# A one-layer GLA and pooling backbone on one core: attention order shifted by half a head, gates broadcast through DRAM, held weight units loaded earlier, modulation products redistributed

## The chip, the cores and the metric

One core of one Trainium2 chip runs the whole program. The metric is device microseconds of an execution, as the median of several runs. The profile is of one execution, and its own time stands beside its span below.

## The reference, cut to what matters

One layer over 256 latent tokens and 256 context tokens of width 2048, all float32:

```
mods (6 x 2048)  = silu(c) @ w_ada + b_ada              (and for c_ctx)
h_lat = x*(1+sc_m) + sh_m;   h_ctx the same with c_ctx
q,k,v,g,a,p,bg   = split(h @ w_in)                      4 heads, HEAD_K 256, HEAD_V 512
o     = gated linear attention, both directions, chunks of 64;
        latent scans start from the context's final states
y_gla = (rmsnorm(o)*gain * silu(g)) @ w_gla_out
y_pool= (grouped (box mean of p - p) @ w_pool_group) * scale @ w_pool_out
mix   = (sigmoid(bg1)*y_gla + sigmoid(bg2)*y_pool) @ w_out
x     = LN(ALPHA*x + gt_m*mix)
ffn   = (silu(z@w1) * (z@w2)) @ w_ffn_out,   z = x*(1+sc_f) + sh_f,   width 5632
out   = LN(ALPHA*x + gt_f*ffn)
```

Only the latent stream is returned. The two gates gt_m and gt_f are rows of 2048 numbers that multiply every token's row.

## The kernel before, in words

Weights come from DRAM in units of 128 x 1024 float32 (512 KB), all issued from SyncE's queue (`raw_unit`, L91), which issues in order. ScalarE rounds a unit to fp32r (`hi`, L97), VectorE takes the rest (`lo`, L98), and TensorE multiplies in three passes: hi by hi, hi by lo, lo by hi. Raw, hi and lo have three buffers each, so weights are prepared up to three units ahead of TensorE. `nat_block` (L143) has the tokens as the stationary operand and two PSUM banks out of the pool "d" of four; a unit is 12 matmuls of 512 columns. `ws_tile` (L116) has the weights as the stationary operand; a unit is 8 matmuls of 512 columns and 8 of 256. Each takes a callback `after` that is called behind each unit: `hooks` (L639) makes one from a table {unit number, counted from 0: what to do}.

The order of instructions on each engine is laid out at build time by a planner, by priority among those whose inputs it reckons to be ready. Priority is the order in which the program issues them, less a bonus inside `tc.high_priority` (the splits of `weights` have 200, the norms 300). `tc.issue_after(i)` keeps an instruction behind i on its engine. On the chip each engine then goes through its list in order.

The stages, with their starts in the profiled execution: modulation and v (0), k of latent and context (233), first q half (331), attention with the g blocks and the p blocks (345 to 590), bg, w_gla_out and w_pool_out in 16 tiles `ct` (590, L737), w_o in four column blocks (907), the FFN's first product in 44 tiles (1019, L901), its second in four column blocks (1500).

Attention: `front(h)` (L479) is a generator with stages between its `yield`s. For direction d it makes decay products (two matmuls L503, ScalarE exponentials, a scan on VectorE, products with k), yields, then products with q (L558 to L564), score matmuls (L571 to L583) and their evacuation, yields, and the same for d = 1. `back(h)` (L604) multiplies the scores with v (L609 to L611), norms with RMS and gates with g (L616 to L622), yields, then transposes o (L628) and evacuates it. For each head the loop (L671) starts the front of h + 1, issues the PV matmuls of h ahead of the g block of h + 1, and lets hooks place the rest: transposes behind unit 1, both remaining stages up to d = 1's k products behind unit 3, the last one behind unit 6.

Modulation products (`ada`, L255): 96 units of w_adaT (512 KB, SyncE's queue, L268), each multiplied with silu(c) on VectorE and summed (L270). `ADA` (L43) says how many are called where: in the modulation stage, behind k tiles (4 each, 3 buffers), in bg tiles (3 each, 2 buffers; the rest behind the last). There are none from the first q half to the end of attention. Behind them `add_mods` fills `fcol`, which holds the gates as columns (128 x 16).

Gates: `bcast_cols` (L780) turns a column form into a tile of 128 x 2048 that has the gate row in every partition: VectorE makes 8 diagonal tiles from the identity (L789), TensorE multiplies each with ones (L791), ScalarE evacuates (L792). It is called behind the first column block of w_o and, for the second gate, in FFN tile 41. `residual` (L808) needs it.

Held blocks: the last column block of w_o (8 units) and the last four units of w_ffn_out are split into buffers of their own and then multiplied part by part (`PARTS`, L823): tokens 0 to 127 first, then tokens 128 to 255 in two halves of 256 columns, so that the norm of the first tokens runs beside the matmuls of the others (`held_block`, L825). Their loads and splits are issued together when the block begins. `rows` (L802) broadcasts the LayerNorm vectors on POOL's queue; the first call stands in the third w_o block.

Of the kernel before, what the change touches and what calls it, by code (L numbers as in the profile page):

```python
# [8 lines left out]
F32 = mybir.dt.float32  # L9
# [33 lines left out]
ADA = ({8: 1, 12: 2}, 4, 3)  # L43
# [15 lines left out]
def trunk(ctx, tc, small, masks, xT, ctxT, x_nat, lnrows, wdec, pmat, c_row,  # L59
# [83 lines left out]
    def nat_block(srcs, acts, k0=0, after=None, last=None, pre=None, cols=None):  # L143
# [20 lines left out]
        return outs  # L164

# [61 lines left out]
    with ExitStack() as c1:  # L227
# [251 lines left out]
        def front(h):  # L479
# [6 lines left out]
            kv = kh.rearrange("p c (t n i) -> p c t n i", t=2, n=2)  # L486
            for d in range(2):
# [67 lines left out]
                yield  # L555
# [48 lines left out]
        def back(h, g, PT, PC):  # L604

            os = [bank("g") for _ in range(2)]
            for t in range(2):
                for j in range(2):
                    PE.matmul(os[t], PC[:, j, t * P:(t + 1) * P], vc[h][:, j, :], start=(j == 0), stop=False)  # L609
                PE.matmul(os[t], PT[:, t, :], vl[h][:, t, :], start=False, stop=False)  # L610
                PE.matmul(os[t], PT[:, 2 + (1 - t), :], vl[h][:, 1 - t, :], start=False, stop=True)  # L611
# [27 lines left out]
        def hooks(at):  # L639

            n = [0]

            def call():
                at.get(n[0], lambda: None)()
                n[0] += 1
            return call

# [38 lines left out]
        ada_pool.append((py, "ra", NRA))  # L686
# [88 lines left out]
    onesf = p2.tile([P, 512], F32, tag="rt", bufs=NRT, name="onesf")[:, :P]  # L775
    V.memset(onesf, 1.0)
    onesq = p2.tile([P, P], F32R, tag="onesq", name="onesq")
    S.activation(onesq, onesf, AF.Copy)

    def bcast_cols(i):  # L780

        gt = p2.tile([P, D], F32, tag="gt", name=nm("gt"))
        fs = p2.tile([P, 2, 16], F32R, tag="fs", name=nm("fs"))
        split(fcol[:, i, :], fs[:, 0, :], fs[:, 1, :])
        for b in range(4):
            o = bank("g")
            for j in range(2):
                dg = p2.tile([P, 4, P], F32R, tag="rt", bufs=NRT, name=nm("dg"))
                V.tensor_tensor(dg, ident.unsqueeze(1).to_broadcast([P, 4, P]),  # L789
                                fs[:, j, 4 * b:4 * b + 4].bitcast(F32).unsqueeze(2).to_broadcast([P, 4, P]), op=ALU.mult)  # L790
                PE.matmul(o, onesq, dg.rearrange("p a b -> p (a b)"), start=(j == 0), stop=(j == 1))  # L791
            S.activation(gt[:, b * 512:(b + 1) * 512], o, AF.Copy)  # L792
# [32 lines left out]
    def held_block(srcs, dst, acts, k0, kend, outs, bst, norm, finish):  # L825

        ws = []
        for src, (hi, lo) in zip(srcs, dst):
            r = raw_unit(src)
            split(r, hi, lo)  # L830
            ws.append((hi, lo))
# [15 lines left out]
    bst = p2.tile([P, 2, 8, 6], F32, tag="bst", name="bst1")  # L847
    for b in range(3):
        outs = nat_block([w_o[8 * b + i] for i in range(8)], m_s)
# [12 lines left out]
    hold = p2.tile([P, 2 * NF, T], F32R, tag="hid", name="hold")  # L862
    hold = hold.rearrange("p a b -> p (a b)")
# [13 lines left out]
    def finish_mix(t):  # L877
        for b in range(4):
# [4 lines left out]
            for j in range(4):  # L883
# [10 lines left out]
    held_block([w_o[24 + i] for i in range(8)],  # L894
               [(hold[:, 2 * U * i:2 * U * i + U], hold[:, 2 * U * i + U:2 * U * i + 2 * U]) for i in range(8)],
               m_s, 0, KT - 1, None, bst, norm_mix, finish_mix)
# [43 lines left out]
    bst = p2.tile([P, 2, 8, 6], F32, tag="bst", name="bst2")  # L940
    for b in range(3):
        outs = nat_block([w_fo[22 * b + i] for i in range(22)], hid_s)
        for t in range(2):
            residual(b, t, outs[t], bst)
# [4 lines left out]
    def finish_ffn(t):  # L949
        mean, rs = mv_rs[t]  # L950
        for b in range(4):
# [6 lines left out]
    outs = nat_block([w_fo[66 + i] for i in range(18)], [hid_s[t] for t, _, _ in PARTS], last=NF - 1,  # L958
                     cols=[c for _, *c in PARTS])
    hold = [hcp.tile([P, 4 * U], F32R, tag="hc", name=nm("hold")) for i in range(2)]  # L960
    held_block([w_fo[84 + i] for i in range(4)],
# [127 lines left out]
```

## Time and profile before

| | |
|---|---|
| time, median of 3 runs | 1768.76 us (1768.55 to 1773.19) |
| profiled execution, its own time | 1772.31 us |
| its span | 1770.5 us |
| TensorE matmul busy | 1730.5 us (98%) |
| VectorE busy | 1170.1 us (66%) |
| ScalarE busy | 800.3 us (45%) |
| GpSimd busy | 11.5 us (1%) |
| mean granted TensorE clock | 0.992 |
| DMA | 393 MB, 222 GB/s over the span |

Times are counted from the first instruction. A matmul's busy time overlaps the next one's, so a busy TensorE is not one at its peak: the distance between two starts tells its pace. An idle time is put down to whatever ended it. A group's "idle before" is the idle time of its engine just ahead of it.

### The profile page before, as it was taken

What the parts mean: (1) busy time and instruction counts of PE and PEld (TensorE: products, weight loads), DVE (VectorE), ACT (ScalarE), POOL (GpSimd) and SP (SyncE); (2) the same over time, 40 slices, a digit from 0 to 9 for tenths busy, and PEclk for the clock granted to TensorE, in tenths of its full rate; (3) what the DMA queues carried; (4) which work ended last, traced back from release to release, by engine and by line L of the source; (5) the groups of instructions that cost most, each with busy time, mean ns of one, the idle gap of its engine ahead of it and who ended that gap; (6) DMA issues with size and microseconds to landing.
All of it is one profiled execution on the core that took longest, in us unless ns stands there. A gap on an engine that the chain in (4) does not pass through costs nothing.

```text
span 1770.5 us, 24390 instructions
## 1 busy us (share of the span) xinstructions
PE 1730.5 (98%) x9407; PEld 1451.1 (82%) x9407; DVE 1170.1 (66%) x1661; ACT 800.3 (45%) x1173; POOL 11.5 (1%) x28
## 2 busy tenths in 40 slices
PE   9999999999999999999999899999999999999996
PEld 5667888887777888888887788888888888888886
DVE  3667866667875677777776756666666666554455
ACT  2223132565874544444444554445444444443332
POOL 0000010000000000000000000000000000000000
PEclk9999999999999999999999999999999999999998
DMA  9797757443334478777785445577777766555553
GB/s 391 292 354 259 258 210 278 159 157 126 110 120 178 157 267 284 267 258 275 278 306 192 155 166 188 186 264 246 248 236 248 233 236 221 192 192 194 196 190 120
DMA packets 109059, 393.26 MB, mean 222 GB/s; under 512 B 12144, under 2 KB 12272, under 8 KB 108432
## 3 DMA queue, kind: packets, MB, share of 16 engines
q1 hardware_dynamic: 107424, 384.25, 62.4%
q0 software_dynamic: 1520, 7.47, 1.2%
q8 instruction: 73, 1.20, 0.3%
q14 instruction: 42, 0.34, 0.1%
HBM read 389.58 MB, written 2.10 MB: 221 GB/s over the span
## 4 chain that ended last, share of the span: by engine, by line
PE 87%; DVE 6%; ACT 3%; DMA 2%; issue 2%; SPq 0%; ACTq 0%; DVEq 0%
PE ps L127 34%; PE ps L131 18%; PE ps L157 10%; PE ps L160 10%; PE ps L158 10%; PE ps L293 2%; DVE lo L98 1%; DMA raw<-in_w_o 1%; ACT hi L97 1%; DMA raw<-in_w_fi 1%; PE ps L581 1%; DMA rw<-in_w_sh_sc 1%; PE ps L571 0%; PE ps L409 0%; PE ps L709 0%
## 5 line engine op out<-in xcount | busy, mean ns | idle before, releaser
L98 DVE TENSOR_TENSOR lo<-raw,hi 128x1024 fp32r<-128x1024 f32 x510 | 623.7, 1224 | 432.9 <-ACT hi L97 420.8
L97 ACT ACTIVATE hi<-raw 128x1024 fp32r<-128x1024 f32 x510 | 539.2, 1058 | 674.0 <-PE ps L127 275.1
L127 PE MATMUL ps<-h,hi 128*128 128x512 f32 x1408 | 353.4, 392 | 0.8 <-DVE h L98 0.8
L127 PEld LDWEIGHTS ps<-h,hi 128*128 128x128 f32 x1408 | 253.3, 189 | 46.5 <-DVE h L98 1.2
L127 PE MATMUL ps<-hl,hi 128*128 128x512 f32 x768 | 210.3, 392 | 0.0
L131 PEld LDWEIGHTS ps<-h,lo 128*128 128x128 f32 x1408 | 192.5, 190 | 13.9
L131 PE MATMUL ps<-h,lo 128*128 128x256 f32 x1408 | 196.8, 282 | 0.0
L127 PEld LDWEIGHTS ps<-hl,hi 128*128 128x128 f32 x768 | 139.4, 189 | 25.3
L157 PE MATMUL ps<-hi,hid 128*128 128x512 f32 (+1 forms) x372 | 134.9, 369 | 0.0
L158 PE MATMUL ps<-hi,hid 128*128 128x512 f32 (+1 forms) x372 | 134.0, 369 | 0.0
L157 PE MATMUL ps<-hi,hl 128*128 128x512 f32 x320 | 128.7, 403 | 2.7 <-ACT hi L97 2.7
L158 PE MATMUL ps<-hi,hl 128*128 128x512 f32 x320 | 126.6, 396 | 0.0
L270 DVE SCALAR_TENSOR_TENSOR ra<-ra,silb 128x1024 f32<-128x1024 f32 x96 | 114.4, 1221 | 13.0 <-DMA ra<-in_w_adaT 12.9
L131 PE MATMUL ps<-hl,lo 128*128 128x256 f32 x768 | 120.5, 282 | 0.0
L131 PEld LDWEIGHTS ps<-hl,lo 128*128 128x128 f32 x768 | 111.7, 190 | 6.9
L160 PE MATMUL ps<-lo,hl 128*128 128x512 f32 x320 | 93.0, 391 | 0.1
L160 PE MATMUL ps<-lo,hid 128*128 128x512 f32 x372 | 90.6, 369 | 0.0
L157 PEld LDWEIGHTS ps<-hi,hid 128*128 128x128 f32 x372 | 69.8, 188 | 12.1 <-DVE xt L812 0.2
L158 PEld LDWEIGHTS ps<-hi,hid 128*128 128x128 f32 x372 | 70.0, 188 | 11.9
L157 PEld LDWEIGHTS ps<-hi,hl 128*128 128x128 f32 x320 | 60.3, 189 | 22.5 <-issue 5.2
L348 DVE TENSOR_TENSOR v<-ps,v 128x512 f32<-128x512 f32 x80 | 50.7, 685 | 39.8 <-PE ps L160 39.7
L160 PEld LDWEIGHTS ps<-lo,hid 128*128 128x128 f32 x372 | 66.2, 188 | 11.9
(259 smaller groups left out, 2045.0 us busy)
## 6 DMA issues: line engine op xcount, KB each, us to landing
raw<-in_w_fi SPq DMA_DIRECT2D x176, 512.0 KB, 4.2
ra<-in_w_adaT SPq DMA_DIRECT2D x96, 512.0 KB, 4.9
raw<-in_w_fo SPq DMA_DIRECT2D x88, 512.0 KB, 4.3
rw<-in_w_sh_sc SPq DMA_DIRECT2D x64, 512.0 KB, 7.4
raw<-in_w_bg SPq DMA_DIRECT2D x64, 512.0 KB, 4.8
raw<-in_w_v SPq DMA_DIRECT2D x32, 512.0 KB, 5.7
raw<-in_w_g SPq DMA_DIRECT2D x32, 512.0 KB, 3.5
raw<-in_w_go SPq DMA_DIRECT2D x32, 512.0 KB, 4.2
```

The costliest lines, as they stand in the source:

```text
L97: S.activation(hi, full, AF.Copy)
L98: last_split[:] = [V.tensor_tensor(lo, full, hi.bitcast(F32), op=ALU.subtract)]
L127: PE.matmul(o, hi[:, j * P:(j + 1) * P], act(n + j), start=(n + j == 0), stop=(n + j == nk - 1), skip_group_check=True)
L131: PE.matmul(o[:, :T], lo[:, j * P:(j + 1) * P], act(n + j)[:, :T], start=False, stop=(n + j == nk - 1), skip_group_check=True)
L157: PE.matmul(o, ah, hi[:, a:b], start=(n + j == k0), stop=False)
L158: PE.matmul(o, al, hi[:, a:b], start=False, stop=False)
L160: last_mm[:] = [PE.matmul(o, ah, lo[:, a:b], start=False, stop=(n + j == end))]
L270: V.scalar_tensor_tensor(r, r, 1.0, silb[half], op0=ALU.mult, op1=ALU.mult, accum_out=mods[:, half, i:i + 1])
L293: mm = PE.matmul(pr[32 * g:32 * g + 32, :256], sil[:, kt, :], r[:, 256 * g:256 * g + 256], start=(u == 0), stop=(u == KT // per - 1), skip ...
L348: V.tensor_tensor(dst, src, dst, op=ALU.add)
L581: PE.matmul(scc[:, t * T:(t + 1) * T], kst[:, c, t * P:(t + 1) * P], q4[:, c].rearrange("p t i -> p (t i)"), start=(d == 0 and c == 0 and ...
```

## The change

- `hooks` moves up; `ADA` gets two more numbers. `ada(1)` is called behind each q tile, `ada(2)` behind the g blocks of heads 1 to 3, out of a buffer of its own (one, in the attention pool). The scan mask becomes bf16 in place of float32.
- `front` yields behind the q products instead of behind the k products (for head 0 behind both), for both directions ahead of the first score matmuls. The loop issues a front's first stage ahead of the g block, its second behind unit 2, the scores of d = 0 behind unit 5, those of d = 1 behind unit 7. PV matmuls are issued behind unit 1 of the g block, transposes behind unit 4.
- `bcast_cols` transposes the 128 x 16 columns on TensorE to 16 x 128, ScalarE evacuates, and two DMAs on POOL's queue write them to DRAM and read them back as a broadcast row into all partitions.
- The eight held units of w_o are loaded and split inside the second and third column block (`b` = 1 and 2, behind units 1, 3, 5, 7 of each), through four staging buffers; `rows(0)` moves behind the held block.
- w_ffn_out holds eight units instead of four: four loaded in its third column block (`b` = 2), four in the fourth, which shortens to 14 units. The last four go to the part of `hid` that the fourth block has read already.

```
-ADA = ({8: 1, 12: 2}, 4, 3)
+ADA = ({8: 1, 12: 2}, 4, 3, 1, 2)
...
                 fold(qT[b][:, i, :], o, HK ** -0.5)
+                ada(ADA[3])
...
+            parts = []
             for d in range(2):
...
-                yield
+                if h == 0:
+                    yield
                 qh = qT[hb][:, 2 * ho:2 * ho + 2, :]
...
+                parts.append((bun, q1, k1, q4, k3, kst, TT, eq))
+                yield
+            for d in range(2):
+                s_ = 1 - d
+                bun, q1, k1, q4, k3, kst, TT, eq = parts[d]
 
                 sc = bank("g")
...
             os = [bank("g") for _ in range(2)]
-            for t in range(2):
-                for j in range(2):
-                    PE.matmul(os[t], PC[:, j, t * P:(t + 1) * P], vc[h][:, j, :], start=(j == 0), stop=False)
...
+            with tc.issue_after(last_mm[0].ins):
+                for t in range(2):
+                    for j in range(2):
+                        PE.matmul(os[t], PC[:, j, t * P:(t + 1) * P], vc[h][:, j, :], start=(j == 0), stop=False)
...
-        ada_pool.clear()
+        ada_pool[:] = [(pg, "ra", 1)]
...
-        mask = pg.tile([P, U], F32, tag="mask", name="mask")
+        mask = pg.tile([P, U], BF16, tag="mask", name="mask")
...
         qT_half(0)
         next(f)
         next(f)
+        next(f)
         st_ = []
-        gs = [g_block(0, hooks({6: lambda: st_.append(run(f))}))]
+        gs = [g_block(0, hooks({1: lambda: next(f), 5: lambda: st_.append(run(f))}))]
         qT_half(1)
         p_blocks = []
         for h in range(H):
             f = front(h + 1) if h + 1 < H else None
+            b = back(h, gs[h], *st_[h])
             if f:
                 next(f)
-            b = back(h, gs[h], *st_[h])
-            next(b)
-            if f:
-                gs.append(g_block(h + 1, hooks({1: lambda: run(b), 3: lambda: (next(f), next(f)),
-                                                6: lambda: st_.append(run(f))})))
+                gs.append(g_block(h + 1, hooks({1: lambda: next(b), 2: lambda: next(f), 4: lambda: run(b),
+                                                5: lambda: next(f), 7: lambda: st_.append(run(f))})))
+                ada(ADA[4])
             else:
-                p_blocks.append(p_block(0, hooks({1: lambda: run(b)})))
+                p_blocks.append(p_block(0, hooks({1: lambda: next(b), 4: lambda: run(b)})))
...
-        ada_pool.append((py, "ra", NRA))
+        ada_pool[:] = [(py, "ra", NRA)]
...
+    pd = ctx.enter_context(tc.tile_pool(name="pd", bufs=2, space=bass.MemoryType.DRAM))
     def bcast_cols(i):
         gt = p2.tile([P, D], F32, tag="gt", name=nm("gt"))
-        fs = p2.tile([P, 2, 16], F32R, tag="fs", name=nm("fs"))
-        split(fcol[:, i, :], fs[:, 0, :], fs[:, 1, :])
-        for b in range(4):
...
-                PE.matmul(o, onesq, dg.rearrange("p a b -> p (a b)"), start=(j == 0), stop=(j == 1))
-            S.activation(gt[:, b * 512:(b + 1) * 512], o, AF.Copy)
+        o = bank("g")
+        PE.transpose(o[:16, :P], fcol[:, i, :], ident)
+        r = p2.tile([16, P], F32, tag="gr", name=nm("gr"))
+        S.activation(r, o[:16, :P], AF.Copy)
+        row = pd.tile([16, P], F32, tag="row", name=nm("row"))
+        nc.gpsimd.dma_start(row, r)
+        nc.gpsimd.dma_start(gt, row.rearrange("a b -> (a b)").partition_broadcast(P))
         return gt
...
+    def held(src, hi, lo, r=None):
+        if r is None:
             r = raw_unit(src)
+        else:
+            nc.sync.dma_start(r, src)
+        with tc.high_priority(PW):
             split(r, hi, lo)
+        return hi, lo
...
+    def hold_next():
+        i = len(held_o)
+        a = 2 * U * i
+        held_o.append(held(w_o[24 + i], hold[:, a:a + U], hold[:, a + U:a + 2 * U], stage[i % 4]))
+
     for b in range(3):
-        outs = nat_block([w_o[8 * b + i] for i in range(8)], m_s)
+        outs = nat_block([w_o[8 * b + i] for i in range(8)], m_s,
+                         after=hooks({i: hold_next for i in range(1, 8, 2)} if b else {}))
...
-        if b == 2:
-            lnr = rows(0)
+            st = hlp.tile([P, 4, U], F32, tag="hl", name="stage")
+            stage += [st[:, i, :] for i in range(4)]
...
+    held_block(held_o, m_s, 0, KT - 1, None, bst, norm_mix, finish_mix)
+    lnr = rows(0)
...
+    slots = [(h, 2 * U * i) for h in hold for i in range(2)] + [(spare, 2 * U * i) for i in range(4)]
...
+        outs = nat_block([w_fo[22 * b + i] for i in range(22)], hid_s,
+                         after=hooks({i: hold_next for i in (4, 9, 14, 19)} if b == 2 else {}))
...
-    outs = nat_block([w_fo[66 + i] for i in range(18)], [hid_s[t] for t, _, _ in PARTS], last=NF - 1,
-                     cols=[c for _, *c in PARTS])
...
+    outs = nat_block([w_fo[66 + i] for i in range(14)], [hid_s[t] for t, _, _ in PARTS], last=NF - 1,
+                     cols=[c for _, *c in PARTS], after=hooks({i: hold_next for i in (7, 9, 11, 13)}))
+    held_block(held_f, hid_s, 28, NF - 1, outs, bst, norm_ffn, finish_ffn)
```

## Rows read from the trace of the kernel before

**Rows 1.** The page's first part: busy us, share of the span, instructions of each engine.

```profile
PE 1730.5 (98%) x9407; PEld 1451.1 (82%) x9407; DVE 1170.1 (66%) x1661; ACT 800.3 (45%) x1173; POOL 11.5 (1%) x28
```

**Rows 2.** Stretches: length, busy us per engine (instructions), clock, DMA share, GB/s.

```profile
345.00:590.00 245.00, 239.69 (x1127) 188.78 (x1126) 171.17 (x262) 156.18 (x290) 2.64 (x7) 1.00 0.40 141
600.00:860.00 260.00, 260.00 (x1499) 229.16 (x1498) 198.32 (x281) 127.28 (x190) 0.00 (x0) 1.00 0.78 264
920.00:1000.00 80.00, 75.07 (x334) 61.19 (x333) 55.16 (x76) 32.67 (x35) 0.53 (x1) 0.96 0.63 214
1740.00:1771.00 31.00, 15.99 (x103) 14.33 (x101) 19.77 (x39) 3.28 (x7) 0.00 (x0) 0.80 0.25 89
```

**Rows 3.** TensorE's waits: us in total, times, longest.

```profile
PE ps L881 <- DVE xt L873: 5.7, 2, 5.1
PE ps L791 <- DVE dg L789: 5.5, 2, 4.2
PE ps L628 <- DVE o L622: 2.8, 3, 1.0
PE ps L571 <- DVE bun L558: 2.5, 3, 1.1
```

**Rows 4.** TensorE's timeline from 907 on: start us, busy us, instruction.

```profile
907.34 0.40 PE L157 MATMUL ps<-hi,mT 128*128 128x512 f32 x1
...
936.87 0.79 PE L791 MATMUL ps<-dg,onesq 128*128 128x512 f32 x1 [4.17 <-DVE dg L789]
...
982.96 0.39 PE L112 MATMUL ps<-hold,mT 128*128 128x512 f32 x1
...
985.90 0.39 PE L113 MATMUL ps<-hold,mT 128*128 128x512 f32 x1
...
1008.77 0.28 PE L114 MATMUL ps<-hold,mT 128*128 128x256 f32 x1
...
1018.63 2.35 PE L127 MATMUL ps<-h,hi 128*128 128x512 f32 x9 [0.79 <-DVE h L98]
...
1492.13 0.50 PE L791 MATMUL ps<-dg,onesq 128*128 128x512 f32 x1 [1.35 <-DVE dg L789]
...
1750.08 0.28 PE L112 MATMUL ps<-hold,hid 128*128 128x256 f32 x1
...
1755.71 0.28 PE L114 MATMUL ps<-hold,hid 128*128 128x256 f32 x1
```

**Rows 5.** Stretches as in rows 2: the first q half, and one head.

```profile
331.00:354.00 23.00, 23.00 (x135) 20.28 (x134) 19.78 (x29) 17.36 (x31) 0.25 (x1) 1.00 0.56 192
...
452.00:492.00 40.00, 38.63 (x177) 28.89 (x176) 34.27 (x57) 31.84 (x66) 0.62 (x2) 1.00 0.31 106
```

**Rows 6.** Modulation products by source line: durations ns min/median/max, first and last start.

```profile
L270 DVE SCALAR_TENSOR_TENSOR ra<-ra,silb x96: 1216/1221/1227, 157.2 to 923.3; 128x1024 f32<-128x1024 f32 x96
```

**Rows 7.** Waits of SyncE's queue: us in total, times, longest.

```profile
SPq L268 <- DVE ra L270: 103.2, 88, 4.5
```

**Rows 8.** Stretches of 5 us, TensorE alone: busy, clock, DMA share, GB/s.

```profile
935.00:940.00 5.00, 3.13 (x7) 0.62 0.64 218
940.00:945.00 5.00, 5.00 (x17) 0.70 0.30 109
```

**Rows 9.** DMA issues: count, KB each, median us to landing.

```profile
ra<-in_w_adaT SPq DMA_DIRECT2D x96, 512.0 KB, 4.9
...
rows<-in_lnrows POOLq DMA_DIRECT2D x4, 1024.0 KB, 11.0
...
out_dram<-xt SPq DMA_DIRECT2D x8, 256.0 KB, 2.3
```

**Rows 10.** The closing products (tile rows): durations ns, first and last start.

```profile
L953 DVE SCALAR_TENSOR_TENSOR xt<-xt,mv,rows x8: 686/750/755, 1753.0 to 1765.0; 128x512 f32<-128x512 f32 x8
L954 DVE SCALAR_TENSOR_TENSOR xt<-xt,stl,rows x8: 740/754/755, 1755.2 to 1765.8; 128x512 f32<-128x512 f32 x8
```

**Rows 11.** A scan of one direction on VectorE: count, busy us, mean ns, idle.

```profile
L513 DVE TENSOR_TENSOR_SCAN bun<-mask,x 128x1024 f32<-128x1024 f32 x1 | 2.3, 2291 | 0.0
```

More of the change, by code (lines that the diff above doesn't have):

```diff
@@ L164, in nat_block, with hooks, call @@
         return outs
+    def hooks(at):
+        n = [0]
+        def call():
+            at.get(n[0], lambda: None)()
+            n[0] += 1
+        return call
     def halves(a, b):
@@ L606, in back @@
             os = [bank("g") for _ in range(2)]
-            for t in range(2):
-                for j in range(2):
-                    PE.matmul(os[t], PC[:, j, t * P:(t + 1) * P], vc[h][:, j, :], start=(j == 0), stop=False)
-                PE.matmul(os[t], PT[:, t, :], vl[h][:, t, :], start=False, stop=False)
-                PE.matmul(os[t], PT[:, 2 + (1 - t), :], vl[h][:, 1 - t, :], start=False, stop=True)
+            with tc.issue_after(last_mm[0].ins):
+                for t in range(2):
+                    for j in range(2):
+                        PE.matmul(os[t], PC[:, j, t * P:(t + 1) * P], vc[h][:, j, :], start=(j == 0), stop=False)
+                    PE.matmul(os[t], PT[:, t, :], vl[h][:, t, :], start=False, stop=False)
+                    PE.matmul(os[t], PT[:, 2 + (1 - t), :], vl[h][:, 1 - t, :], start=False, stop=True)
             st = pg.tile([P, 3, 2], F32, tag="st", bufs=2, name=nm("st"))
@@ L637, in back @@
             og[h] = o4
[L639 to L646, printed above, removed]
         kT_half(0)
@@ L823, in trunk, with held_block @@
     PARTS = ((0, 0, 512), (1, 0, 256), (1, 256, 512))
-    def held_block(srcs, dst, acts, k0, kend, outs, bst, norm, finish):
-        ws = []
-        for src, (hi, lo) in zip(srcs, dst):
+    def held(src, hi, lo, r=None):
+        if r is None:
             r = raw_unit(src)
+        else:
+            nc.sync.dma_start(r, src)
+        with tc.high_priority(PW):
             split(r, hi, lo)
-            ws.append((hi, lo))
+        return hi, lo
+    def held_block(ws, acts, k0, kend, outs, bst, norm, finish):
         for p, (t, c0, c1) in enumerate(PARTS):
@@ L847, in trunk @@
     bst = p2.tile([P, 2, 8, 6], F32, tag="bst", name="bst1")
+    hold = p2.tile([P, 2 * NF, T], F32R, tag="hid", name="hold")
+    hold = hold.rearrange("p a b -> p (a b)")
+    held_o = []
+    stage = []
+    def hold_next():
+        i = len(held_o)
+        a = 2 * U * i
+        held_o.append(held(w_o[24 + i], hold[:, a:a + U], hold[:, a + U:a + 2 * U], stage[i % 4]))
     for b in range(3):
-        outs = nat_block([w_o[8 * b + i] for i in range(8)], m_s)
+        outs = nat_block([w_o[8 * b + i] for i in range(8)], m_s,
+                         after=hooks({i: hold_next for i in range(1, 8, 2)} if b else {}))
         if b == 0:
@@ L892, in finish_mix @@
             split(tmp.rearrange("p (k t) -> p k t", t=P), d[:, :, 0, t * P:(t + 1) * P], d[:, :, 1, t * P:(t + 1) * P])
-    held_block([w_o[24 + i] for i in range(8)],
-               [(hold[:, 2 * U * i:2 * U * i + U], hold[:, 2 * U * i + U:2 * U * i + 2 * U]) for i in range(8)],
-               m_s, 0, KT - 1, None, bst, norm_mix, finish_mix)
+    held_block(held_o, m_s, 0, KT - 1, None, bst, norm_mix, finish_mix)
+    lnr = rows(0)
     h2g = halves(*h2)
@@ L940, in trunk, with hold_next @@
     bst = p2.tile([P, 2, 8, 6], F32, tag="bst", name="bst2")
+    hold = [hcp.tile([P, 4 * U], F32R, tag="hc", name=nm("hold")) for i in range(2)]
+    spare = hid.rearrange("p k s t -> p (k s t)")
+    slots = [(h, 2 * U * i) for h in hold for i in range(2)] + [(spare, 2 * U * i) for i in range(4)]
+    held_f = []
+    def hold_next():
+        h, a = slots[len(held_f)]
+        held_f.append(held(w_fo[80 + len(held_f)], h[:, a:a + U], h[:, a + U:a + 2 * U]))
     for b in range(3):
-        outs = nat_block([w_fo[22 * b + i] for i in range(22)], hid_s)
+        outs = nat_block([w_fo[22 * b + i] for i in range(22)], hid_s,
+                         after=hooks({i: hold_next for i in (4, 9, 14, 19)} if b == 2 else {}))
         for t in range(2):
@@ L957, in trunk @@
     mv_rs = {}
-    outs = nat_block([w_fo[66 + i] for i in range(18)], [hid_s[t] for t, _, _ in PARTS], last=NF - 1,
-                     cols=[c for _, *c in PARTS])
-    hold = [hcp.tile([P, 4 * U], F32R, tag="hc", name=nm("hold")) for i in range(2)]
-    held_block([w_fo[84 + i] for i in range(4)],
-               [(hold[i // 2][:, 2 * U * (i % 2):2 * U * (i % 2) + U],
-                 hold[i // 2][:, 2 * U * (i % 2) + U:2 * U * (i % 2) + 2 * U]) for i in range(4)],
-               hid_s, 36, NF - 1, outs, bst, norm_ffn, finish_ffn)
+    outs = nat_block([w_fo[66 + i] for i in range(14)], [hid_s[t] for t, _, _ in PARTS], last=NF - 1,
+                     cols=[c for _, *c in PARTS], after=hooks({i: hold_next for i in (7, 9, 11, 13)}))
+    held_block(held_f, hid_s, 28, NF - 1, outs, bst, norm_ffn, finish_ffn)
 def _score_masks(np):
```

11 lines of the change are left out of this document (removed).

## The prediction

> **What bounds the kernel now.** I read the page's first part, then busy time by stage, then TensorE's waits, then its timeline in the stages the diff touches. TensorE is busy 1730.5 of 1770.5 us [rows 1], so the whole reserve is some 40 us, and what can be won lies in the gaps, plus the matmuls taken out and those that ran at a lower clock. The start (the modulation and v stages) holds a good part of the gaps and the change doesn't touch it. The rest: attention (345 to 590) is idle 245 - 239.7 = 5.3 us, all of it in two kinds of wait, the o transposes on the norm's product (L628, 2.8) and the score matmuls on the q product (L571, 2.5) [rows 2, 3]. The w_o stage has the wait of the gate's broadcast (L791, 4.2 of its 5.5 us there) and that for the normed x before the second set of transposes (L881, 5.1) [rows 3, 4]. The last 31 us hold 16.0 of TensorE work: the end is a chain on VectorE and the stores [rows 2]. So: a matmul-bound kernel with a dozen short stalls, and each edit aims at some of them.
>
> A full-width matmul follows the last after (985.90 - 982.96)/13 = 0.226 us, a 256-column one after (1755.71 - 1750.08)/47 = 0.120 us [rows 4]. A unit of weights is 12 full matmuls = 2.71 us in a nat block and 8 + 8 = 2.77 us in a ws tile.
>
> **Attention moved by half a head.** No matmul is added. The PV matmuls move behind the second unit of the gate block, the o transposes behind the fifth: three units (8.1 us) instead of two (5.4) for the norm, which now comes at most 1.0 us late [rows 3]; that wait should go. The q products come a stage earlier (before the block, and behind unit 3), the scores behind units 6 and 8. The first set then has far over the 1.1 us by which it is late now; the second has five units (13.6 us) for all its elementwise work and may stay late. What is against it is VectorE: 34.3 us busy in the head from 452 to 492 [rows 5], and each of three heads now takes two modulation products, 2 x 1.22 = 2.4 us [rows 6], so 36.7 in a head that would last 38.6 without stalls. Bounds: everything goes, -5.3; VectorE keeps its present 5.7 us of idle time per head, so a head takes 36.7 + 5.7 = 42.4 instead of 40, +7.2 over three. I take half the gain, -2.7, since the half-head shift hands VectorE two independent pieces to fill its idle time with.
>
> In the first q half VectorE is busy 19.8 of 23 us [rows 5], and four products add 4.9: 1.7 us over. It costs nothing while the first head's scores, which now stand two units into the gate block, give it 5.4 us of room; +1.7 if not. The bf16 mask: a scan takes 2.29 us [rows 11]; a gain of up to half of that in eight scans, or nothing. I take nothing; VectorE is not the bound of the sum.
>
> **Modulation products spread.** 14 of the 48 units that the bg stage now takes (three per tile, what is left after the last) move: one per q tile (8), two per gate block of heads 1 to 3 (6). With three per tile the other 34 end in the twelfth of 16 tiles, so no load or product of them is left when w_o begins. In the stage they leave, TensorE has no gap (600 to 860 in [rows 2]), so that gives nothing itself; it makes the gate's columns ready early.
>
> **Gate through DRAM, w_o stage.** From the first w_o matmul to the first held one: 982.96 - 907.34 = 75.6 us. 3 blocks x 8 units x 12 matmuls x 0.226 = 65.1, so 10.5 is lost. It falls into the 4.2 us wait at L791, eight replicating matmuls (8 x 0.226 = 1.8), a granted clock of 0.62 and 0.70 in the ten microseconds behind the wait ((0.38 + 0.30) x 5 = 3.4, the lower level is 1.2 GHz) [rows 4, 8], and 1.1 of small late splits. The wait goes because nothing on TensorE needs VectorE's diagonal tiles any more; one transpose (0.12) replaces eight matmuls, its input ready for tens of microseconds. With the wait the clock drop goes. VectorE loses eight 512-wide products and gets four held splits (4.9 us) in each of the second and third column block. The price is latency: a store to DRAM (nearest row: output stores, 2.3 us) and then a broadcast load of 1 MB (the row of the LayerNorm vectors, same shape and queue, 11.0) [rows 9], 13.3 us in series on POOL's queue, past which only a broadcast of c and, later, the LayerNorm rows are queued. The first block ends at about 907.3 + 21.7 = 929, so the gate lands at about 943; it is needed before the third block wants the first one's banks back, at 951. I take -9.0; bounds -10.5 and, with a new wait (first rival), -0.4. The Trainium skill ("DMA: Bandwidth & Descriptors", Anatomy of one DMA — SWDGE (gpsimd) path) puts a DMA at 2.0 us plus its bytes over 436 GB/s: about 2.0 + 4.4 = 6.4 us here, an estimate by that page. The rows say twice that, which speaks against the change where the page would not; by the page the first rival falls away.
>
> **Kept units ahead (mix).** The eight held loads come out of the end of the stage: from 982.96 to the last held matmul, 1008.77 + 0.12, are 25.9 us for 48 x 0.226 + 96 x 0.120 + 16 transposes at 0.120 = 24.3. 1.6 is lost to a late held split and to the first transposes, and I take -1.6 (bounds 0 and -3, the latter if VectorE, with its splits done early, also shortens the 9.7 us from there to the FFN's first matmul at 1018.63). The 5.1 us wait for the second half's norm stays: residual, statistics and scaling still follow the last matmul. The LayerNorm rows, 2 MB, now load in this stage instead of at 899; the FFN needs them in its fifth tile, 16 x 2.77 = 44 us in.
>
> **Gate of the FFN.** Eight matmuls (1.8) and the wait of 1.35 us at L791 [rows 4] go, 0.1 for a transpose comes: -3.1 (bounds -1.8 if the transpose waits for VectorE's last product instead, and -3.2). Its DRAM trip has some 60 us of cover, the first w_fo block.
>
> **Eight kept at the end.** Matmuls stay the same. The first row half ends 96 x 0.120 = 11.5 us before the last matmul instead of 5.8. Of the 16 closing products of about 0.7 us (eight per line, from 1753.0 to 1765.8), three had begun when TensorE ended at 1756.0 [rows 4, 10]. With all eight of the first half done by then, five of the 13 leave the tail: -3.5, of which I give back 0.7 for the rstd chain that they covered: -2.8 (bounds -3.5, -1.5). The four loads that overwrite spent parts of hid wait for matmuls long past.
>
> **Sum:** -2.7 - 9.0 - 1.6 - 3.1 - 2.8 = -19.2. On the profiled execution, 1772.3 (its span and 1.8 around it), that is 1753.1; this execution was 3.5 above the median of the three runs shown, 1768.76, so the forecast for a median is 1750.
>
> **Rivals.**
> 1. *The gate comes late.* VectorE takes its instructions in order. If the first residual is queued before the gate has landed, every later split stands behind it for up to 13.3 us, and TensorE has three units (8.1 us) ahead: 5.2 us of stall, and 3.4 for the clock again: 1758. For it: the rows' 13.3. Against: other splits are ahead of it by priority. With 14 us until 943, it decides when more than 8.1 are waited out.
> 2. *VectorE bounds attention*: +7.2 in place of -2.7, about 1760. For it: 36.7 of 38.6. Against: five units of room.
> 3. *The change moves stalls and doesn't remove them*: scores, transposes and the residual wait anew, and only the 16 matmuls (3.6) and the tail (2.8) are won: 1762.
> 4. *Slower: the single buffer for modulation loads stops the load queue.* SP issues in order; a load into that buffer waits for the previous product, and weight loads stand behind it. Landing 4.9 us [rows 9] and a product of 1.2 make 6.1 per q tile of 2 x 2.77 = 5.5. If the product also waits behind two splits and a scan on VectorE (2 x 1.2 + 2.3, and its neighbours), a cycle is 12: each half loses 4 x 6.5 less the 8.1 that is loaded ahead, together 36: 1786. It outweighs the gains from a cycle of about 9.9. Against it: with two to four buffers SP waited 103.2 us in 88 times for these products, 1.2 each, at most 4.5 [rows 7], and no TensorE gap came of it.
> 5. *All terms at their ends*: 1743.
>
> **Numbers.** Forecast 0.50 (own range 1745 to 1756), the rivals 0.17, 0.15, 0.08, 0.05, 0.05 in order. The range 1742 to 1762 leaves out rival 4, half of 3 and 5, and the tail of 2. About 0.3% (5.3 us) can be told from no change: faster means under 1763.5. That holds all of the forecast, rivals 1 and 5, nearly all of 2 and half of 3: 0.87; same 0.08; slower 0.05.
>
> **What would show it.** Right: no L791 and no clock drop near 935; w_o stage of about 66.6 us; no L628 wait; VectorE over 90% in the heads; some 8 us between the last matmul and the last closing product. Wrong: an idle VectorE ended by the gate's DMA, a TensorE wait on a split behind it, L571 waits that stay at three, or weight splits waiting for loads in the q tiles.

## The result, and the profile after

The changed kernel takes 1756.88 us (median of four runs, 1753.73 to 1759.65) against 1770.03 for the kernel before on the same chip: ratio 0.9919, 95% interval [0.9899, 0.9938]. The forecast was 1750, with an own range of 1745 to 1756 and a wider one, rivals included, of 1742 to 1762. The profiled execution was the fastest of the four, 1753.73; its page and its answers to [rows 1] and [rows 2, 5] (stretches, columns as there) read:

```profile
PE 1724.2 (98%) x9393; PEld 1446.5 (83%) x9393; DVE 1160.0 (66%) x1642; ACT 795.1 (45%) x1164; POOL 13.7 (1%) x32
```

```profile
338.00:583.00 245.00, 245.00 (x1166) 195.23 (x1166) 192.17 (x297) 160.07 (x297) 2.64 (x7) 1.00 0.49 171
452.00:491.00 39.00, 39.00 (x181) 29.80 (x180) 35.98 (x60) 31.19 (x65) 0.62 (x2) 1.00 0.39 134
935.00:940.00 5.00, 5.00 (x24) 4.14 (x23) 3.52 (x5) 2.12 (x3) 0.00 (x0) 1.00 0.68 223
940.00:945.00 5.00, 5.00 (x24) 4.14 (x23) 5.00 (x8) 2.12 (x2) 0.82 (x2) 1.00 0.56 202
```

The attention stretch shows no idle TensorE (245.00 of 245.00), VectorE is busy 35.98 of 39 us in a head (92%), and the clock around 940 stays at 1.00 where [rows 8] had 0.62 and 0.70. TensorE's largest waits, the answer to [rows 3]:

```profile
PE ps L897 <- DVE xt L889: 5.6, 2, 5.2
PE ps L157 <- ACT hi L97: 3.6, 3, 1.4
PE ps L160 <- DVE lo L98: 1.7, 1, 1.7
```

The waits on the diagonal tiles, on o and on the q product are gone. The timeline at the borders of the stages, as in [rows 4], and the closing products, as in [rows 10]:

```profile
900.80 0.40 PE L157 MATMUL ps<-hi,mT 128*128 128x512 f32 x1
...
967.48 0.40 PE L112 MATMUL ps<-hold,mT 128*128 128x512 f32 x1
...
992.25 0.28 PE L114 MATMUL ps<-hold,mT 128*128 128x256 f32 x1
...
1002.23 0.96 PE L127 MATMUL ps<-h,hi 128*128 128x512 f32 x3 [0.78 <-DVE h L98]
...
1494.09 0.39 PE L157 MATMUL ps<-hi,hid 128*128 128x512 f32 x1
...
1740.16 0.28 PE L114 MATMUL ps<-hid 128*128 128x256 f32 x1
```

```profile
L978 DVE SCALAR_TENSOR_TENSOR xt<-xt,mv,rows x8: 740/744/746, 1731.7 to 1744.6; 128x512 f32<-128x512 f32 x8
L979 DVE SCALAR_TENSOR_TENSOR xt<-xt,stl,rows x8: 729/742/746, 1734.6 to 1747.2; 128x512 f32<-128x512 f32 x8
```

From such starts follow the stages. The row for w_ffn_out before also rests on this one:

```profile
1514.20 0.40 PE L157 MATMUL ps<-hi,hid 128*128 128x512 f32 x1
```

The fourth column is a second profiled execution of the same program (the first experiment):

| stage, us | before | after | after, again | change forecast | change measured |
|---|---|---|---|---|---|
| first v matmul to first of w_o (attention) | 887.62 | 880.74 | 880.91 | -2.7 | -6.9, -6.7 |
| w_o blocks 1 to 3 | 75.62 | 66.68 | 71.15 | -9.0 | -8.9, **-4.5** |
| held w_o (mix) | 25.81 | 24.77 | 24.76 | -1.6 | -1.0 |
| to the FFN's first matmul | 9.86 | 9.98 | 9.97 | 0 | +0.1 |
| FFN, first product | 495.57 | 491.86 | 491.90 | -3.1 | -3.7 |
| w_ffn_out, to the last matmul | 241.51 | 246.07 | 246.06 | 0 | **+4.6** |
| last matmul to the end | 14.7 | 11.8 | 11.8 | -2.8 | -2.9, -3.0 |

So the sum of -19.2 met -18.5 in one execution and -14.8 in the next (from span to span, so with some tenths of a us ahead of the first row), by terms that missed in both directions. The stages leave two questions: what costs 4.6 us in w_ffn_out, which in its first two blocks runs the same instructions as before, and why the w_o stage came out 4.5 us apart in two executions of one program.

### The profile page after: what moved, and what is told of

Same layout as the page of the kernel before. It is cut to its first block, busy times and chain, and to the rows that moved or that the text cites. A ratio compares the mean times of both kernels' runs of the same rounds, so it can differ in the third digit from the quotient of the medians.

```text
span 1752.0 us, 24330 instructions
## 1 busy us (share of the span) xinstructions
PE 1724.2 (98%) x9393; PEld 1446.5 (83%) x9393; DVE 1160.0 (66%) x1642; ACT 795.1 (45%) x1164; POOL 13.7 (1%) x32
## 4 chain that ended last, share of the span: by engine, by line
PE 94%; DVE 2%; DMA 2%; issue 1%; ACT 1%; SPq 0%; DVEq 0%; POOL 0%; ACTq 0%; POOLq 0%
PE ps L127 35%; PE ps L131 18%; PE ps L157 11%; PE ps L158 10%; PE ps L160 10%; PE ps L302 2%; PE ps L598 1%; PE ps L114 1%; PE ps L113 1%; PE ps L112 1%; PE ps L627 1%; DMA rw<-in_w_sh_sc 1%; DVE lo L98 1%; PE ps L588 0%; DMA raw<-in_w_o 0%
## 5 line engine op out<-in xcount | busy, mean ns | idle before, releaser
L157 PE MATMUL ps<-hi,hid 128*128 128x512 f32 (+1 forms) x348 | 129.2, 376 | 0.0
L158 PE MATMUL ps<-hi,hid 128*128 128x512 f32 (+1 forms) x348 | 128.6, 376 | 0.0
L279 DVE SCALAR_TENSOR_TENSOR ra<-ra,silb 128x1024 f32<-128x1024 f32 x96 | 114.7, 1220 | 11.2 <-DMA ra<-in_w_adaT 11.1
L157 PEld LDWEIGHTS ps<-hi,hid 128*128 128x128 f32 x348 | 65.5, 188 | 13.0 <-DVE xt L815 0.2
L158 PEld LDWEIGHTS ps<-hi,hid 128*128 128x128 f32 x348 | 65.5, 188 | 12.8
```

The lines of the kernel that those rows point to most:

```text
L157: PE.matmul(o, ah, hi[:, a:b], start=(n + j == k0), stop=False)
L158: PE.matmul(o, al, hi[:, a:b], start=False, stop=False)
L279: V.scalar_tensor_tensor(r, r, 1.0, silb[half], op0=ALU.mult, op1=ALU.mult, accum_out=mods[:, half, i:i + 1])
```

## Experiments

Each ran beside the kernel before on the same chip. Not all ran on one chip; the medians of the kernel before beside them were 1770.56 (experiments 1 to 4), 1771.03 (5 to 8), 1770.85 (9 to 11) and 1771.40 (12), so experiments are also compared with each other. Pace means the mean distance between starts of 512-column matmuls of a stage that follow each other without a wait.

**1. The changed kernel again.**

> The changed kernel unchanged, for its scatter and a second profile. Theory P (the place of the tile hid in SBUF sets the pace of the matmuls that read it): full matmuls of the w_ffn_out stage again 232 to 233 ns apart, where the w_o stage has 227; stage from the first w_ffn_out matmul to the last matmul about 246 us. Rival R (the slow pace belongs to that one execution, a chip or clock effect): 227 this time and about 241.5 us. Time 1753 to 1760 by either.

Measured: 1759.39 us (1756.53 to 1760.5), ratio 0.9934 [0.9922, 0.9947]. The w_ffn_out pace is again 232.3 ns (before: 227.2), the stage 246.06: rival R falls. And the w_o stage is 71.15. VectorE's timeline there shows why (start, us, instruction, idle before):

```profile
933.22 1.22 DVE L98 TENSOR_TENSOR lo<-raw,hi 128x1024 fp32r<-128x1024 f32 x1
940.75 0.70 DVE L814 TENSOR_TENSOR ps<-ps,gt 128x512 f32<-128x512 f32 x1 [6.31 <-DMA gt<-row]
941.36 1.22 DVE L98 TENSOR_TENSOR lo<-raw,hi 128x1024 fp32r<-128x1024 f32 x1
```

The first residual stands in VectorE's list ahead of a split, and VectorE sits 6.3 us until the gate has landed. TensorE's timeline and the stretches behind it:

```profile
939.92 0.39 PE L158 MATMUL ps<-hi,mT 128*128 128x512 f32 x1
942.63 1.60 PE L160 MATMUL ps<-lo,mT 128*128 128x512 f32 x4 [2.32 <-DVE lo L98]
```

```profile
940.00:945.00 5.00, 2.68 (x9) 1.90 (x8) 4.25 (x6) 2.12 (x2) 0.00 (x0) 0.82 0.28 99
945.00:950.00 5.00, 5.00 (x20) 4.04 (x19) 5.00 (x8) 2.12 (x2) 1.04 (x2) 0.84 0.54 161
```

That is 2.3 us of wait and (0.18 + 0.16) x 5 = 1.7 of clock, together 4.0 of the 4.5 us by which the stage is longer. In the first execution the same two places read:

```profile
934.39 1.22 DVE L98 TENSOR_TENSOR lo<-raw,hi 128x1024 fp32r<-128x1024 f32 x1
937.09 0.70 DVE L814 TENSOR_TENSOR ps<-ps,gt 128x512 f32<-128x512 f32 x1 [1.48 <-DMA gt<-row]
```

There the gate landed 3.7 us earlier, and TensorE felt nothing. The gate's two transfers (KB, us to landing), here and then in the first execution:

```profile
gt<-row POOLq DMA_DIRECT2D x1, 1024.0 KB, 9.3
...
row<-gr POOLq DMA_DIRECT2D x1, 8.0 KB, 5.3
```

```profile
gt<-row POOLq DMA_DIRECT2D x1, 1024.0 KB, 6.2
...
row<-gr POOLq DMA_DIRECT2D x1, 8.0 KB, 5.0
```

14.6 and 11.2 us for the pair, beside the 13.3 that [rows 9] had given. The estimate of 6.4 us by the Trainium skill ("DMA: Bandwidth & Descriptors", Anatomy of one DMA — SWDGE (gpsimd) path) is met by neither. In both executions the DMA engines were 98 to 101% busy from 925 to 935 and 67 or 68% from 935 to 940.

**2 and 3. The place of hid in memory.** In the built program the tile `hid` (and `hold`, its memory in the w_o stage) starts at byte 134400 of each partition before, a multiple of 256, and at 121472 after, 128 past one, since other tiles are allocated ahead of it. The other operands of the matmuls that read it (`hi`, `lo` and `mT`) start at the same multiples of 256 in both kernels and in the padded ones.

```
     bst = p2.tile([P, 2, 8, 6], F32, tag="bst", name="bst1")
+    pad = p2.tile([P, 32], F32, tag="pad", name="pad")      # 128 bytes
+    V.memset(pad, 0.0)
     hold = p2.tile([P, 2 * NF, T], F32R, tag="hid", name="hold")
```

> The changed kernel with 128 bytes of padding ahead of hid, which moves it from address 121472 to 121600 in each partition, now a multiple of 256 bytes as it was in the kernel before (134400). No other instruction differs but one small memset. Theory P in its form of alignment: w_ffn_out pace back to 227 ns, the stage 241.5 us, the held w_o matmuls 227 in place of 233, together 4.8 us less than the changed kernel. Rival P2 (it is the region of memory that hid lies in, not its alignment): pace stays at 232. Rival R: no difference beyond scatter.

> The kernel before with the same 128 bytes ahead of hid, which moves it from 134400 to 134528, no longer a multiple of 256. Theory P (alignment): w_ffn_out pace 232 to 233 ns in place of 227 and the held w_o matmuls 233, 4.5 to 4.8 us slower than the kernel before. Rivals P2 and R: 227 and no difference.

Measured: the changed kernel with the padding 1752.25 us (1749.37 to 1753.05), 0.9895 [0.9881, 0.9908]; the kernel before with it 1775.02, 1.0027 [1.0017, 1.0037]. First and last matmul of w_ffn_out on TensorE's timeline, the changed kernel padded, then the kernel before padded:

```profile
1497.43 0.40 PE L157 MATMUL ps<-hi,hid 128*128 128x512 f32 x1
...
1738.83 0.28 PE L114 MATMUL ps<-hid 128*128 128x256 f32 x1
```

```profile
1511.18 0.39 PE L157 MATMUL ps<-hi,hid 128*128 128x512 f32 x1
...
1757.35 0.28 PE L114 MATMUL ps<-hold,hid 128*128 128x256 f32 x1
```

241.40 and 246.17 us, paces 227.1 and 232.5: the padding mends the one and spoils the other by the same amount. Theory P holds in its form of alignment, P2 falls, since the tile moved by only 128 bytes. The held w_o matmuls, which stream from the same memory, go from 233.2 to 226.7 and from 227.5 to 232.7.

**4. The gates back on TensorE.** `bcast_cols` of the kernel before in the changed one.

> The changed kernel with the gates' broadcast undone: eight diagonal products on VectorE and eight replicating matmuls in place of the transpose and the two DMAs; hid stays off a multiple of 256 bytes (126080). Theory G (most of the w_o stage's gain is the gate's: its wait, its matmuls and the clock drop behind the wait): the wait for the diagonal products is back with about 4 us, the clock falls behind it, the w_o stage is 74 to 76 us in place of 66.7, and the FFN stage 3 us longer: 10 to 12 us slower than the changed kernel. Rival A (the modulation products spread over attention have made the gate's columns ready early, so that the matmul broadcast waits for nothing): only the matmuls return, 2 x 1.8 us, and some late splits: 4 to 5 us slower.

Measured: 1762.38 us, 0.9957 [0.9943, 0.9970], 3.0 slower than experiment 1. The wait for the diagonal tiles is back with 2.54 us, and the clock behind it falls to 0.79 and 0.87:

```profile
PE ps L800 <- DVE dg L798: 2.5, 1, 2.5
```

```profile
925.00:930.00 5.00, 2.46 (x7) 1.67 (x6) 4.85 (x6) 2.70 (x5) 0.00 (x0) 0.79 0.97 351
930.00:935.00 5.00, 5.00 (x20) 4.00 (x19) 4.08 (x6) 4.07 (x5) 0.00 (x0) 0.87 0.84 299
```

Yet the w_o stage is 71.4 us, the same as experiment 1's 71.2; the FFN is 494.2 (+2.3). So the DRAM route took away the wait at TensorE and, in experiment 1's execution, put one of like price at VectorE; in the first execution VectorE's 1.5 us cost TensorE nothing. Neither theory's number came: the wait of theory G is back, at 2.5 us in place of 4, and the price of 3.0 us lies below A's 4 to 5. And against the kernel before, the stage is 4.2 us shorter (75.6 to 71.4) without the DRAM route too. Of that, 1.6 lie in a shorter wait and 1.7 in the clock behind it. VectorE makes the first diagonal tile at 906.5 here and made it at 926.6 before, where the last modulation product stood at 923.3; the old broadcast without the spread products was not tried.

**5. The gate early.** On the padded kernel; the columns are ready at 830, the transpose waited for the first w_o block.

```
+    gt = bcast_cols(0)
     for b in range(3):
         outs = nat_block([w_o[8 * b + i] for i in range(8)], m_s, ...)
         if b == 0:
...
-            gt = bcast_cols(0)
```

> The changed kernel with the 128 bytes of padding of the run before, and with the first gate's broadcast called ahead of the first w_o block instead of behind it: nothing else differs. In the second execution of the changed kernel VectorE sat idle 6.3 us in front of the first residual for the gate's DMA, TensorE then waited 2.3 us for a split queued behind it and the granted clock fell to 0.82. The gate's columns have been ready since 830 us. Theory L (this queueing behind a late gate is the whole difference between 66.7 and 71.1 us of w_o stage, and what scatters from run to run): no VectorE wait for the gate, stage 65.5 to 66.5 us, 3.5 to 5 us below the padded kernel (1752.25), runs closer together. Rival M (VectorE and the weight loads are late there for other reasons, the gate only ends the wait): stage stays at 69 to 71 us and the time within 1 us of the padded kernel.

Measured: 1751.97 us (1750.32 to 1752.83), 0.9888 [0.9876, 0.9901]; stage 69.77, the padded kernel's 69.69. The wait for the gate is gone from VectorE, but theory L's gain did not come: TensorE now waits later and longer for a weight split whose load is late.

```profile
948.79 1.07 PE L160 MATMUL ps<-lo,mT 128*128 128x512 f32 x4
952.23 0.50 PE L157 MATMUL ps<-hi,mT 128*128 128x512 f32 x1 [2.37 <-ACT hi L97]
```

The DMA queues from 941 to 952 (packets, MB, share of the 16 engines) and the issues in it:

```profile
q0 software_dynamic: 288, 2.10, 45.4%
q1 hardware_dynamic: 525, 1.91, 43.0%
...
rows<-in_lnrows POOLq DMA_DIRECT2D x2, 1024.0 KB, 7.7
raw<-in_w_o SPq DMA_DIRECT2D x3, 512.0 KB, 8.8
```

The 2 MB of LayerNorm rows, issued when the staging buffers fall free at 941, take nearly half of the engines' time, and a unit of weights lands after 8.8 us (4.2 without them, experiment 10). The Trainium skill ("DMA: Bandwidth & Descriptors", Queues, rings and completion order) says that each DMA engine takes turns between the queues that have work; the 45.4 to 43.0% agree.

**6. No products in attention.** `ADA` ends in `0, 0`.

> The changed kernel with no modulation products in attention (both new numbers of ADA are 0), so that the bg stage takes all 48 again. Theory S (the spread is what makes the gate's columns ready early; in the kernel before the last product stood at 923): products run to about 920 again, the gate's store leaves some us later, VectorE waits longer for the gate, the w_o stage is 74 to 78 us in place of 71.1: 3 to 6 us slower than the changed kernel. Rival T (the gate's way is set by the end of the first w_o block alone): w_o stage 71 and no difference. For attention: products off VectorE gain nothing if it isn't the bound there (start to the last pooling matmul 562.1 us as now); if VectorE bounded it, attention would shorten by up to 2.4 us a head.

Measured: 1760.22 us (1759.57 to 1761.45), 0.9937 [0.9925, 0.9949], 0.8 over experiment 1 and within its scatter. The last product stands at 913 in place of 826, the gate's store leaves at 926.1 in place of 925.8, the w_o stage is 72.7 (experiment 1: 71.2). Rival T is nearer: the end of the first w_o block sets the gate's way. Attention is 562.1 us with the products as without.

**7 and 12. Attention's old order, with the products (7) and without (12).** The edit, cut; in 12 `ADA` ends in `0, 0` as well.

```
...
             for d in range(2):
...
-                if h == 0:
-                    yield
+                yield
...
-                gs.append(g_block(h + 1, hooks({1: lambda: next(b), 2: lambda: next(f), 4: lambda: run(b),
-                                                5: lambda: next(f), 7: lambda: st_.append(run(f))})))
+            b = back(h, gs[h], *st_[h])
+            next(b)
+                gs.append(g_block(h + 1, hooks({1: lambda: run(b), 3: lambda: (next(f), next(f)),
+                                                6: lambda: st_.append(run(f))})))
...
```

> The changed kernel with attention's old order (yields, PV matmuls, transposes and hooks as before); the spread of the modulation products and the bf16 mask stay. Theory O (the order is the whole gain in attention): start to the last pooling matmul 569 us in place of 562.1, the waits on the norm's product and on the q product are back, three each, 6.5 to 7 us slower than the changed kernel. Rival V (with the products added, VectorE's load makes the old order worse than it was): more than 7 us slower, up to 14. Rival B (the bf16 mask or the spread gave part of it): less than 5 us slower.

> The changed kernel with attention's old order and no modulation products in attention; the bf16 mask stays. With the old order and the products, start to the last pooling matmul took 579.6 us, against 568.8 in the kernel before and 561.9 with the new order, with products or without. Theory W (in the old order the products are what costs the 10.8 us, since the chains on VectorE that TensorE waits for grow by each product put among them): 568 to 569 us. Rival B (the bf16 mask or the new memory layout changed attention too): 565 to 567 if the mask gains, 571 or more if something else of the change slows the old order. Time of the whole: about 1765 to 1767 by theory W.

Measured: 1776.22 us with the products (1.0024 [1.0010, 1.0038]), 1766.77 without (0.9977 [0.9968, 0.9987]). From the first v matmul to the last pooling matmul:

| us | without products | with |
|---|---|---|
| old order | 568.75 (kernel before: 568.81) | 579.60 |
| new order | 562.11 | 562.10 |

TensorE's waits in experiment 7, then in experiment 12, the group of [rows 3] (L581 and L584 are score matmuls, L638 the o transpose):

```profile
PE ps L581 <- DVE bun L568: 4.7, 3, 2.5
PE ps L584 <- DVE bun L571: 3.7, 1, 3.7
PE ps L638 <- DVE o L632: 2.9, 3, 1.1
```

```profile
PE ps L638 <- DVE o L632: 2.8, 3, 1.0
PE ps L581 <- DVE bun L568: 2.5, 3, 1.1
```

Without the products the old order has the very waits of [rows 3] again. So the order is the whole gain in attention, and the mask, seen in the old order, gives nothing (theory W). Rival V was right in kind for experiment 7, and its "up to 14" was too low for the 17.5 us by which attention grew against the new order: in the old order the products cost 10.9 us, in the new one none. They cost time where TensorE already waited for the chain that they lengthen, and none where it did not.

**8. Four units kept at the end.**

> The changed kernel with four units kept at the end of w_ffn_out in place of eight, loaded and split at the end, as in the kernel before. Theory E (the closing products of the first half now fit behind the longer second half): from the last matmul to the end 14.7 us in place of 11.8, 2.9 us slower than the changed kernel. Rival F (the tail is set by the second half's chain of residual, statistics, products and stores, so the number kept is nothing beyond some small amount): within 1 us. The pace of the stage stays at 232 ns in both, since hid stays where it is.

Measured: 1761.12 us (1757.18 to 1762.93), 0.9937 [0.9923, 0.9950]. From the last matmul to the end 14.5 us in place of 11.8: theory E, with 2.7 us. This execution's FFN was 2.2 us longer too, which three versions without this edit show too (last section).

**9 and 10. The LayerNorm rows late.** On the padded kernel, in 10 with the early gate as well:

```
     held_block(held_o, m_s, 0, KT - 1, None, bst, norm_mix, finish_mix)
+    keep = p2.tile([P, 8], F32, tag="keep", name="keep")
+    with tc.issue_after(last_split[0].ins):
+        V.tensor_tensor(keep, st[:, 3, 0:8], st[:, 2, 0:8], op=ALU.add)
     lnr = rows(0)
```

> The changed kernel with the 128 bytes of padding, and with the staging buffers kept in use until the normed x has been transposed (one small sum on VectorE reads them there), so that the LayerNorm rows, which take the same memory, load near 1005 in place of 941 to 955. The gate's broadcast stays behind the first w_o block. Theory N (the 2 MB of LayerNorm rows meet the third block's weight loads and make the late first weight split near 950, which costs 1.1 to 2.6 us and sometimes the clock behind it): that wait is gone, the one for the gate (1.2 to 2.5 us near 940) stays; w_o stage 67 to 68.5 in place of 69.7 to 71.1 us, 1.5 to 2.5 us below the padded kernel. Rival Q (the weight loads are late there because the whole stage asks for more than the DMA engines move): the wait stays, w_o stage 69.5 to 71.

> Both: the gate's broadcast ahead of the first w_o block, and the LayerNorm rows behind the held block. Theory L and N together (two late things in the stage, the second hidden behind the first, which is why the early gate alone won nothing): no wait of TensorE left from 900 to 967, w_o stage 65.3 to 66, 3.5 to 4.5 us below the padded kernel (1752.25): about 1748. Rival Q: the wait near 950 stays at 2 us or more and the stage near 69.

Measured: 1749.14 us (1748.37 to 1751.08), 0.9874 [0.9858, 0.9891], and 1749.59 (1747.38 to 1751.56), 0.9878 [0.9863, 0.9892]: 3.1 and 2.7 us below the padded kernel, the fastest versions, not told apart by time. The w_o stage: 67.10 and 65.68, against 69.69 (neither edit) and 69.77 (gate alone). The padded kernel's wait behind the rows, then what is left in 9, which is the gate's wait, then the ends of the stage in 10, in which TensorE waits for nothing:

```profile
957.29 0.50 PE L157 MATMUL ps<-hi,mT 128*128 128x512 f32 x1 [1.90 <-ACT hi L97]
```

```profile
942.28 1.19 PE L160 MATMUL ps<-lo,mT 128*128 128x512 f32 x4 [0.95 <-DVE lo L98]
```

```profile
901.32 0.47 PE L157 MATMUL ps<-hi,mT 128*128 128x512 f32 x1
...
967.00 0.39 PE L112 MATMUL ps<-hold,mT 128*128 128x512 f32 x1
```

In 10 a unit of weights lands in 4.2 us where experiment 5 had 8.8:

```profile
raw<-in_w_o SPq DMA_DIRECT2D x4, 512.0 KB, 4.2
```

Theory N holds: the rows out of the way, the stage is 2.6 us shorter and the kernel 3.1 us faster. The price of the rows isn't a fixed one: in experiment 4 they are issued at 946 too, and TensorE waits for no split there. Theory L as recorded, that the late gate is the whole difference, fell with experiment 5. What is left of it is small: with the rows in the way, the early gate won nothing; without them it won 1.4 us of stage, in one profiled execution each, which the medians do not show.

**11. Another offset.** 64 bytes of padding, hid at 121536, 192 past a multiple of 256.

> The changed kernel with 64 bytes of padding ahead of hid: address 121536, 192 over a multiple of 256 bytes. So far the tile was fast at two addresses that are multiples of 256 and slow at three that are 128 over one. If any offset from 256 costs alike: pace of the w_ffn_out matmuls 232 to 233 ns. If the number of pieces that a row of 512 bytes touches is what counts, also 232 to 233; if smaller steps cost more: over 234. If only an offset of 128 is bad: 227.

Measured, one execution: 1754.18 us. Where hid is the stationary operand (w_ffn_out) the pace is 229.0 ns, where it streams (held w_o) 233.3. None of the three outcomes: the price depends on the offset and on the operand's part.

## Why the prediction was right and where it failed

The direction and the wider range of 1742 to 1762 held. The median of 1756.88 stands 7 us over the forecast, 0.9 outside the forecast's own range and next to the 1758 of the first rival. That it came so near the rival's number is luck: of the rival's 8.6 us no more than 4.0 came in one execution and none in the other, while a term that nobody had forecast (w_ffn_out) added 4.6 and attention gave 4 more than was taken.

- **Attention, -2.7 forecast, -6.9 and -6.7 measured.** The mechanism was right, the size was not. I took half of the listed waits because VectorE would be 95% busy. It is 92% busy and TensorE waits nowhere: in the new order VectorE's products come early enough, with the modulation products or without (experiments 6, 7 and 12). Nor was -5.3 the bound. A listed wait is idle time only, and the matmul ahead of it counts as busy for 0.39 us, where the next would have started after 0.23. So each of the six waits costs 0.16 us more than is listed: the six matmuls started 6.3 us late, 5.3 of it listed. The last 0.4 of the 6.7 is not traced.
- **w_o, -9.0 forecast, -8.9 in the first execution, -4.5 in the second.** The step that failed is "the gate lands at about 943; it is needed before the third block wants the first one's banks back, at 951". It landed at 937 to 941, and was needed sooner: by VectorE's order, as the first rival had it. So the route through DRAM by itself won 0.2 to 4.7 us of the stage and not 9.0; 4.2 were there without it (experiment 4). The rival's price was 5.2 + 3.4; the measured one 2.3 + 1.7. The rival gave TensorE 8.1 us of prepared units as cover. VectorE's idle times for the gate of 2.7, 3.5, 4.5, 5.9 and 6.3 us (experiments 2, 9, 12, 6, 1) cost TensorE waits of 1.2, 1.0, 2.4, 3.2 and 2.3, so the cover was 1.5 to 4.0 us in these; why it was no more stays open. The LayerNorm rows were costed at nothing ("now load in this stage"), and they were the second wait, 1.0 us in the first execution and up to 2.4 in experiment 5 (cause: experiments 9 and 10).
- **Mix, -1.6 forecast, -1.0 measured.** Of the missing 0.6, the place of `hold` in memory costs 24.77 - 24.52 (experiment 2) = 0.25; the rest is not traced.
- **FFN gate, -3.1 forecast, -3.7 measured.** The eight matmuls of the broadcast had stood 281 ns apart before, not 226, which is 0.4 of the 0.6.
- **Tail, -2.8 forecast, -2.9 and -3.0 and, by experiment 8, -2.7 measured.** The closing products of L979 end at 1747.9, 7.5 us behind the last matmul.
- **w_ffn_out, not in the sum, +4.6 measured.** The sum has no term for the memory layout, which the change moves. With other tiles ahead of it hid moved by 12928 bytes, off its multiple of 256, and the stage's 924 matmuls of 512 columns at 232.3 - 227.2 = 5.1 ns each make 4.7 (experiments 2 and 3).
- **Rivals.** The first came in part (w_o). The fourth did not: SyncE waited 30 us for products between 320 and 600, and no gap of TensorE followed. The second did not come either, but in the old order the products cost 10.9 us.

In the profiled execution the terms that missed cancelled, by luck (-18.5 against -19.2). A single profile would have shown the w_o step as right; the second execution did not.

## What to carry to other kernels

After a change of tiles, compare the pace of matmuls that did not change, and the addresses of their operands: 128 bytes moved 4.5 us here. A transfer that takes the place of a wait at TensorE can become a wait at the engine that uses it first, as the gate's did at VectorE; start it when its input is ready, not where the old code stood, and look which other transfers the freed buffers release into the same microseconds. Extra work on an engine costs by the slack of the chain that it joins: the same products cost 10.9 us in one order and nothing in the other, with VectorE 92% busy in the second.

## What the runs showed of the hardware

- The start of an fp32r operand in SBUF changes TensorE's pace: with `hid` as the stationary operand 227 ns for 512 columns at two starts that are multiples of 256 bytes (121600, 134400), 232 at three that are 128 past one (121472, 126080, 134528), and 229 at one that is 192 past (121536); streaming from it 227, 233 and 233.3. Other offsets were not tried, and why is open.
- Behind the 5.2 us wait at L897 the FFN's first matmuls run 427 ns apart for some four microseconds in four of the fourteen profiled executions (experiments 7, 8, 9, 12) and at 230 in the others, for 1.6 to 2.2 us. The granted clock in experiment 8, then in experiment 1:

```profile
1000.00:1005.00 5.00, 3.62 (x16) 3.28 (x16) 3.03 (x10) 3.13 (x7) 0.00 (x0) 0.56 0.00 0
1005.00:1010.00 5.00, 4.22 (x11) 3.33 (x11) 2.66 (x6) 2.54 (x7) 0.00 (x0) 0.50 0.00 0
```

```profile
1000.00:1005.00 5.00, 3.48 (x16) 3.24 (x16) 3.02 (x10) 3.12 (x7) 0.00 (x0) 0.66 0.00 0
1005.00:1010.00 5.00, 4.02 (x22) 3.46 (x22) 3.04 (x7) 4.04 (x10) 0.00 (x0) 1.00 0.00 0
```

TensorE did the same before in both; 0.50 is the lower level, 1.2 GHz. The clock falls near this wait in all fourteen executions; what differs is whether it is back at 1.00 when the FFN's first matmuls start. With the gate's landing this may be what scatters the runs by some 4 us, which is not shown: only the profiled executions can be looked at.
